# Hybrid SSD/GLA decoder trunk on one core: projecting z of two groups, and values of two heads, in one pass 512 columns wide

## The chip, the core and the metric

The kernel runs on one core of a Trainium2 chip. The core has a matrix engine (TensorE, in the profile PE; its loads of stationary operands are PEld), a vector engine (VectorE, DVE), an activation engine (ScalarE, ACT), a general engine (GpSimd, POOL) and SyncE (SP), which here only issues transfers. Matrix products land in PSUM, which has eight banks; a bank holds 128 rows of 512 float32 numbers. The metric is device time in microseconds of one execution; the figure for a kernel is the median over runs.

## The reference

One decoder layer over 2048 tokens of width 1024, with 16 learned meta tokens put in front. Everything is float32.

```python
u = rmsnorm(h, norm_w)
z, xbc, dt_raw, q, k, v, g_gla, a_lr, merge_g = split_cols(u @ w_in, IN_WIDTHS)
# SSD branch: 4 groups of 4 heads, scan over chunks of 128 tokens
xbc = silu(causal_depthwise_conv(xbc))           # x, B, C
y   = ssd_chunked(x, softplus(dt_raw + dt_bias), -exp(a_log), B, C) + d_skip * x
y_ssd = rmsnorm_per_group(y * silu(z))           # z: 1024 columns, 256 per group
# GLA branch: 4 heads, keys of 128, values of 256, decay per key channel
log_a = log_sigmoid(a_lr @ gla_gate_w2 + gla_gate_b) / 16
y_gla = rmsnorm_per_head(gla_chunked(q / sqrt(128), k, v, log_a)) * silu(g_gla)
# merge
merged = sigmoid(g1) * (y_ssd @ w_branch[0]) + sigmoid(g2) * (y_gla @ w_branch[1])
out = rmsnorm(h + merged @ w_out)[:, 16:]
```

Both scans carry a state from chunk to chunk; the meta tokens' chunk sets the first state. What the change touches is the projection of z (a 2048 x 1024 product with a 1024 x 1024 matrix, then z * sigmoid(z) up to a factor) and of v (the same size).

## The kernel before

**Arithmetic.** A float32 product is made of three products of float32r operands: each operand is split into a high part and a rest, and `accum` (L183 to L187) issues high x high, high x rest and rest x high into one PSUM bank. So every product appears in the profile as three matmuls, on L185, L186 and L187.

**Stages.** The tokens are cut into four blocks of 512 (block 0 carries the 16 meta tokens too). For each block, eight units run in order: `ssd_proj` for SSD groups 0 to 3, then `gla_proj` for GLA heads 0 to 3. After the blocks come gate, branch and output products (`Stage`), which the change doesn't touch.

**Two forms of projection.** `proj_feat` puts the result's channels on the 128 rows: the stationary operand is a 128 x 128 weight tile, the moving one 512 tokens; 24 matmuls of 512 columns for 128 channels (in block 0, some go as two halves of 264). `proj_tok` puts tokens on the rows: the stationary operand is 128 tokens of `u`, the moving one a strip of weights. For z of groups 1 to 3 and for the values of each head the strip is 256 columns wide, the four token tiles of a block share two banks of the pool `pj` (`halves_of`), and the work is 96 matmuls. Group 0's z goes with the small dt and decay columns, 288 wide, in five (block 0) or four banks taken from three pools. In block 0 the values also need the meta tokens' rows, a fifth tile, in a bank of `pt`.

**PSUM.** Eight banks in three pools: `pj` 3 (projections, the gates' matmuls), `pt` 3 (transposes, sums), `pc` 2 (the scans' products). A tile is taken by `bank(pool, tag)`; if all of a pool's banks are in use, the instruction that first writes the new tile waits until the last reader of an older one is done.

**Order.** While the blocks run, the order on PE and SP is that of the program text (`manual_schedule`); the order on DVE, ACT and POOL is chosen by the framework's planner. Each projection unit is a generator. At each of its `yield`s the loop at L852 calls `step()`, which advances every running generator by one call: SSD scans (`ssd_scan`, eight calls, nine in block 0), GLA scans (`gla_scan`, eleven calls), `dt_chain`, `gates` (seven calls; it makes the GLA decays, with two matmuls on L434 in its second and fifth call), the next block's `load_u`, and a unit that adds up operands for the later products. So a block is 48 steps: a piece of projection, then one call of everything that runs beside it. A scan begins when the unit that feeds it has ended (`begin`). Before, `gates` begins with unit 1.

**In a scan's call.** An SSD call (`before`, `after`) takes a `pt` bank for three transposes, then a `pc` bank `py` and a second `pc` bank `pst`; `py` is free after L575 on DVE, `pst` after L570. A GLA scan takes two `pt` banks at once for its sums (fifth call), `pt` for transposes (second, sixth and tenth; L816 is the tenth, L817 on DVE frees its banks), `pc` banks for the products of two levels in several calls (L703, freed by L710) and for `po` in the seventh and eighth (L799 to L801, freed by L806 on ACT).

**The end of the blocks.** The last head's scan (block 3, head 3) begins as soon as its values are projected, ahead of the head's two output-gate projections, with `last=True`: it transposes its keys in its sixth call rather than the second. When the projections have run out, the loop over `k` steps the scans that are left, and puts between the steps the first work of the gate products (`between`).

Of the kernel before, what the change touches and what calls it, by code (L numbers as in the profile page):

```python
# [14 lines left out]
P = 128  # L15
D = 1024
KT = 8
META = 16
# [8 lines left out]
NT4 = 5  # L27
# [13 lines left out]
def trunk_kernel(ctx: ExitStack, tc: tile.TileContext, xm, xmt, w_feat, w_tok, w_zm, w_br, w_o,  # L41
# [303 lines left out]
    def new_block(b, u):  # L345
# [14 lines left out]
        o.alr = mk(bpool, [P, 5, 48], F32, "alr")  # L360
        o.mov = lambda kt, a, n: tuple(t[:, kt, a:a + n] for t in u)
# [3 lines left out]
    def dt_chain(o, psd):  # L365
# [12 lines left out]
        e = t80("de")  # L378
        nc.scalar.activation(e, x, AF.Abs)
        nc.scalar.activation(e, e, AF.Exp, scale=-1.0)  # L380
        w1 = t80("dw")
        nc.vector.tensor_scalar(w1, e, 1.0, None, op0=ALU.add)
        ln = t80("dl")
# [66 lines left out]
    def ssd_proj(o, g):  # L450
        m0, tt = o.m0, o.tt
        feats = []
        zs = mk(wk, [P, NCH, 256], F32, "tok4", bufs=NT4)
        if g == 0:
            pss = [bank(*pl) for pl in [(pj, "pj")] * 3 + [(pt, "pt")] + ([(pc, "pc")] if m0 else [])]
            yield from proj_tok("zm", w_zm, o.u, o.starts + [0] * o.ci0, list(enumerate(pss)), 288, 1, 256)
            begin(dt_chain(o, pss[NCH:] + pss[:NCH]))
            done = [(ps[:, :256], zs[:, c]) for c, ps in enumerate(pss[:NCH])]
# [7 lines left out]
        yield  # L466
# [138 lines left out]
    def gla_proj(o, h):  # L605
        m0 = o.m0
# [6 lines left out]
        for ps, (a, n) in zip(proj_feat(f"g{t0 + 1}", w_feat[t0 + 1], o.segs_all, o.mov), o.segs_all):  # L613
            nc.scalar.activation(kf[:, a:a + n], ps[:, :n], AF.Copy)
        yield
        vh = mk(wk, [P, NCH, 256], F32R, "tok4", bufs=NT4)
        vl = mk(wk, [P, NCH, 256], F32R, "tok4", bufs=NT4)
        vm = None
        pss, places = halves_of(pj, "pj")
        if m0:  # L620
            vm = mk(wk, [P, 256], F32, "c1", bufs=NC1)[:META]
            pv5 = bank(pt, "pt")
            places.append((2, pv5[:, :256]))
        yield from proj_tok(f"v{h}", w_tok[SG + h], o.u, o.starts + [0] * o.ci0, places)

        last, gs = (o.b, h) == (nblk - 1, GH - 1), []
        if last:
            begin(gla_scan(o, h, qs, kf, (vh, vl), vm, gs, True))
        if m0:
            nc.scalar.activation(vm, pv5[:META, :256], AF.Copy)  # L630
        for r, ps in enumerate(pss):
            split(*[t[:, 2 * r:2 * r + 2].rearrange("p c f -> p (c f)") for t in (vh, vl)], ps)
        yield
        for j in range(2):
# [6 lines left out]
        if not last:  # L641
            begin(gla_scan(o, h, qs, kf, (vh, vl), vm, gs))
# [182 lines left out]
    def begin(gen):  # L825
        begun.append(gen)
# [322 lines left out]
def _layout(inputs):  # L1149
# [26 lines left out]
    w_tok = tiles(np.concatenate([cols(o_z, 1024), cols(o_v, 1024)], axis=1), 256)  # L1176
# [34 lines left out]
    return {"xm": xm, "xmt": xmt, "w_feat": w_feat, "w_tok": w_tok, "w_zm": w_zm, "w_br": w_br, "w_o": w_o, "cf32": cf32, "cmsk": cmsk.reshape(P, -1),  # L1211
# [21 lines left out]
```

## Time and profile before

| | |
|---|---|
| median of 3 runs | 2332.01 us (2328.81, 2332.01, 2332.72) |
| profiled execution, span | 2327.3 us, granted TensorE clock 0.988 |
| PE busy | 2247.1 us (97%), 12641 matmuls |
| PEld busy | 1956.3 us (84%) |
| DVE busy | 1550.3 us (67%) |
| ACT busy | 1184.8 us (51%) |
| POOL busy | 684.6 us (29%) |
| transfers | 518.05 MB, mean 223 GB/s |

Each profile row gives start or total times of one engine, line and operation. The page gives no time of the profiled execution other than its span, from the first to the last instruction; the span is 4.7 us under the median of the runs, and sums are made against the span and carried over to the median. Matmuls are pipelined, so that their modelled durations overlap; two rows' starts tell how far apart they ran. Blocks 0 to 3 begin near 14, 416, 779 and 1141 us by their first 288-wide rows; the projections end near 1494 us, and the products after the blocks run alone from about 1550 us.

### The profile page before, as it was taken

To read this page: it belongs to the slowest core of one execution; us is meant where nothing else is said; L and a number is where in the kernel's file an instruction comes from. 1 tells how busy PE (TensorE), PEld (TensorE's weight loads), DVE (VectorE), ACT (ScalarE), POOL (GpSimd) and SP (SyncE) were. 2 spreads that over 40 slices of the span, in tenths; PEclk is the share of its full clock that TensorE was granted. 3 is DMA by queue.
4 is the path that set the end of the run, shared out by engine and by line. 5 is a ranking of instruction groups with operands and counts; after the bars stand their busy time and mean duration, and the time that the engine had idled before them with its cause. 6 is when DMAs were issued, how large, how long until landed. Compare 5 with 4: busy or idle time off the path is not lost. (4 is left out here: it accounts for less than half of the span.)

```text
span 2327.3 us, 36519 instructions
## 1 busy us (share of the span) xinstructions
PE 2247.1 (97%) x12641; PEld 1956.3 (84%) x12641; DVE 1550.3 (67%) x2895; ACT 1184.8 (51%) x2758; POOL 684.6 (29%) x681
## 2 busy tenths in 40 slices
PE   7899999999999999999999999889999999999998
PEld 7899888888888989898988898768888888888776
DVE  5676766676675666566568555654588954788766
ACT  4666655465544455544465443554554545554443
POOL 3344433122221122212122100037324264324331
PEclk9999999999999999999999999989999999999999
DMA  8766865767785666786677655457577866687743
GB/s 302 230 204 208 292 228 205 223 199 237 244 284 181 214 213 217 255 270 215 194 230 214 206 168 162 145 178 247 186 255 268 305 227 216 231 286 259 243 145 122
DMA packets 301545, 518.05 MB, mean 223 GB/s; under 512 B 27696, under 2 KB 143664, under 8 KB 301360
## 3 DMA queue, kind: packets, MB, share of 16 engines
q1 hardware_dynamic: 200400, 402.84, 53.0%
q10 hardware_dynamic: 100960, 112.88, 14.1%
q8 instruction: 99, 1.62, 0.3%
q14 instruction: 86, 0.70, 0.1%
HBM read 368.42 MB, written 147.19 MB: 222 GB/s over the span
## 5 line engine op out<-in xcount | busy, mean ns | idle before, releaser
L185 PE MATMUL pj<-u,whl 128*128 128x512 f32 (+1 forms) x1184 | 449.0, 379 | 14.6 <-ACT acc L475 6.7
L187 PE MATMUL pj<-u,whl 128*128 128x512 f32 (+1 forms) x1184 | 433.5, 366 | 1.4 <-POOL whl L166 0.8
L186 PE MATMUL pj<-u,whl 128*128 128x512 f32 (+1 forms) x1184 | 432.0, 365 | 0.0
L185 PE MATMUL pj<-whl,u 128*128 128x256 f32 (+1 forms) x992 | 289.0, 291 | 2.4 <-ACT u L298 1.5
L187 PE MATMUL pj<-whl,u 128*128 128x256 f32 (+1 forms) x992 | 282.4, 285 | 1.6 <-DVE u L300 1.6
L186 PE MATMUL pj<-whl,u 128*128 128x256 f32 (+1 forms) x992 | 282.2, 284 | 1.0 <-POOL whl L166 1.0
L185 PEld LDWEIGHTS pj<-u,whl 128*128 128x128 f32 x1184 | 226.8, 192 | 53.7 <-ACT acc L475 7.7
L185 PE MATMUL pj<-b,a 128*128 128x512 f32 x640 | 254.0, 397 | 13.8 <-ACT sn L945 7.6
L187 PEld LDWEIGHTS pj<-u,whl 128*128 128x128 f32 x1184 | 226.0, 191 | 38.0 <-POOL whl L166 1.9
L186 PEld LDWEIGHTS pj<-u,whl 128*128 128x128 f32 x1184 | 227.0, 192 | 33.6
L187 PE MATMUL pj<-b,a 128*128 128x512 f32 x640 | 252.2, 394 | 0.0
L186 PE MATMUL pj<-b,a 128*128 128x512 f32 x640 | 251.0, 392 | 0.0
L185 PEld LDWEIGHTS pj<-whl,u 128*128 128x128 f32 x992 | 189.7, 191 | 4.0 <-ACT u L298 1.8
L187 PEld LDWEIGHTS pj<-whl,u 128*128 128x128 f32 x992 | 189.6, 191 | 2.3 <-DVE u L300 2.3
L80 POOL TENSOR_TENSOR wr<-wr 128x256 f32<-128x256 f32 x80 | 66.3, 829 | 425.0 <-DMA wr<-u 174.7
L186 PEld LDWEIGHTS pj<-whl,u 128*128 128x128 f32 x992 | 189.9, 191 | 1.6 <-POOL whl L166 1.2
L166 POOL TENSOR_TENSOR whl<-wr,whl 128x512 fp32r<-128x512 f32 (+1 forms) x100 | 134.7, 1355 | 187.4 <-ACT whl L165 151.5
L904 DVE TENSOR_TENSOR b<-br,b 128x512 fp32r<-128x512 f32 x196 | 154.9, 808 | 44.7 <-ACT b L903 43.5
L919 POOL TENSOR_TENSOR as<-ar,ar 128x512 f32<-128x512 f32 x40 | 60.0, 1499 | 411.3 <-DMA ar<-in_w_br 197.3
L479 DVE SCALAR_TENSOR_TENSOR acc<-cin,hcw,acc 128x512 f32<-128x512 f32 (+1 forms) x192 | 154.4, 804 | 30.9 <-ACT acc L475 29.8
L929 DVE TENSOR_TENSOR a<-ar,a 128x512 fp32r<-128x512 f32 x160 | 126.3, 797 | 67.2 <-ACT a L928 64.4
L903 ACT ACTIVATE b<-br 128x512 fp32r<-128x512 f32 x196 | 119.4, 626 | 99.0 <-DMA br<-br_t 38.6
(274 smaller groups left out, 5068.8 us busy)
## 6 DMA issues: line engine op xcount, KB each, us to landing
whl<-k_s SPq DMA_DIRECT2D x96, 512.0 KB, 4.5
whl<-k_g SPq DMA_DIRECT2D x96, 512.0 KB, 4.2
whl<-k_v SPq DMA_DIRECT2D x48, 512.0 KB, 3.7
whl<-k_z SPq DMA_DIRECT2D x36, 512.0 KB, 3.8
wr<-in_w_feat SPq DMA_DIRECT2D x64, 256.0 KB, 4.5
k_s<-whl SPq DMA_DIRECT2D x32, 512.0 KB, 3.6
cb<-cumd ACTq DMA_DIRECT2D x64, 256.0 KB, 5.8
y<-gg ACTq DMA_DIRECT2D x64, 256.0 KB, 4.5
```

Source lines behind the costliest of these rows:

```text
L80: nc.gpsimd.tensor_tensor(o, x, y, op=ALU.subtract)
L166: nc.gpsimd.tensor_tensor(hl[:, 1], raw, hl[:, 0].bitcast(F32), op=ALU.subtract)
L185: nc.tensor.matmul(ps, sh, mh, start=first, stop=False, **kw)
L186: nc.tensor.matmul(ps, sh, ml, start=False, stop=False, **kw)
L187: nc.tensor.matmul(ps, sl, mh, start=False, stop=last, **kw)
L479: nc.vector.scalar_tensor_tensor(acc, cin[:, k:k + tt], hcw[:, ti, k:k + 1], acc, op0=ALU.mult, op1=ALU.add)
L903: nc.scalar.activation(t[:, 0], raw, AF.Copy)
L904: nc.vector.tensor_tensor(t[:, 1], raw, t[:, 0].bitcast(F32), op=ALU.subtract)
L919: nc.gpsimd.tensor_tensor(s1, a21, a22, op=ALU.add)
L929: nc.vector.tensor_tensor(t[:, 1], src, t[:, 0].bitcast(F32), op=ALU.subtract)
```

## The change

Z of groups 1 and 2 is projected in unit 1, 512 columns wide, into four banks (three of `pj`, one of `pt`); unit 2 has then no z projection. Group 3's z stays 256 wide. The values of heads 0 and 1 are projected in unit 4, those of heads 2 and 3 in unit 6, in the same way; in block 0 the meta tokens' tile takes a bank of `pc`. `proj_tok` yields after each quarter of a wide projection. The four tiles are read out 256 columns at a time, as each bank holds two groups or heads. A block still has 48 steps: the units have 6, 8, 4, 6, 8, 4, 8 and 4 of them in place of six each. `gates` begins with unit 2. The scan of heads 1 and 3 transposes its keys in the sixth call in every block. In block 3, the scan of head 2 begins after its values, then head 3's query and key are projected, its scan begins, and the output gates of both heads (four projections) come last. The weights' strips are laid out anew for this on the host (`w_pair`, `w_z3`), with as many bytes and loads as before. `tok4` gets a sixth buffer; five small tiles per block have one buffer in place of two, and `dt_chain` uses three of them as scratch; the meta tokens' values wait in the state tile `s_gla`.

```diff
-NT4 = 5
+NT4 = 6
...
         for q0 in range(0, nq, 2):
-            if q0 == nq // 2:
+            if q0 and (q0 == nq // 2 or width == 512):
                 yield
...
+    def token_banks(m0):
+        return [bank(*pl) for pl in [(pj, "pj")] * 3 + [(pt, "pt")] + ([(pc, "pc")] if m0 else [])]
...
-            setattr(o, nm, mk(bpool, [P, 5, NH], F32, nm, bufs=2))
+            setattr(o, nm, mk(bpool, [P, 5, NH], F32, nm))
...
     def ssd_proj(o, g):
...
+        elif g == 1:
+            pss = token_banks(0)
+            yield from proj_tok("z1", w_pair[0], o.u, o.starts, list(enumerate(pss)), 512, 1)
+            o.zs.update({i: mk(wk, [P, NCH, 256], F32, "tok4", bufs=NT4) for i in (1, 2)})
+            done = [(ps[:, i * 256:(i + 1) * 256], o.zs[1 + i][:, c]) for c, ps in enumerate(pss) for i in range(2)]
+        elif g == 3:
+            pss, places = halves_of(pj, "pj")
+            yield from proj_tok("z3", w_z3, o.u, o.starts, places)
+            zs = o.zs[3] = mk(wk, [P, NCH, 256], F32, "tok4", bufs=NT4)
+            done = [(ps, zs[:, 2 * r:2 * r + 2].rearrange("p c f -> p (c f)")) for r, ps in enumerate(pss)]
         else:
-            pss, places = halves_of(pj, "pj")
-            yield from proj_tok(f"z{g}", w_tok[g], o.u, o.starts, places)
-            done = [(ps, zs[:, 2 * r:2 * r + 2].rearrange("p c f -> p (c f)")) for r, ps in enumerate(pss)]
+            done = []
+        zs = o.zs[g]
         for ps, dst in done:
             nc.scalar.activation(dst, ps, AF.Tanh, scale=0.5)
             nc.vector.scalar_tensor_tensor(dst, dst, 1.0, ps, op0=ALU.add, op1=ALU.mult)
-        yield
+        if done:
+            yield
...
+    def gla_values(o, h):
+        m0 = o.m0
+        vs = [[mk(wk, [P, NCH, 256], F32R, "tok4", bufs=NT4) for _ in range(2)] for _ in range(2)]
+        vms = [s_gla[:META, h + i] for i in range(2)]
+        pss = token_banks(m0)
+        yield from proj_tok(f"v{h}", w_pair[1 + h // 2], o.u, o.starts + [0] * o.ci0, list(enumerate(pss)), 512, 1)
+        for c, ps in enumerate(pss[:NCH]):
+            for (vh, vl), i in zip(vs, range(2)):
+                split(vh[:, c], vl[:, c], ps[:, i * 256:(i + 1) * 256])
+        for i in range(2):
+            if m0:
+                nc.scalar.activation(vms[i], pss[NCH][:META, i * 256:(i + 1) * 256], AF.Copy)
+            o.vals[h + i] = vs[i], vms[i]
+        yield
...
+    def gla_proj(o, h):
+        end = o.b == nblk - 1 and h >= GH - 2
+        gs = o.gs.setdefault(h, [])
+        if not end or h == GH - 2:
+            yield from gla_keys(o, h)
+        if h % 2 == 0:
+            yield from gla_values(o, h)
+        if end and h == GH - 2:
+            begin(gla_scan(o, h, *o.gla[h], *o.vals[h], gs))
+            yield from gla_keys(o, h + 1)
+            begin(gla_scan(o, h + 1, *o.gla[h + 1], *o.vals[h + 1], o.gs.setdefault(h + 1, []), True))
+        yield from gla_out_gates(o, h, o.gs[h])
+        if not end:
+            begin(gla_scan(o, h, *o.gla[h], *o.vals[h], gs, h % 2 == 1))
...
-            if i == 1:
+            if i == 2:
                 begin(gates(o))
```

`gla_keys` (query and key projections, two steps) and `gla_out_gates` (two output-gate projections, two steps) are the parts of the old `gla_proj` under names of their own.

More of the change, by code (lines that the diff above doesn't have):

```diff
@@ L614, in gla_proj, with gla_out_gates @@
             nc.scalar.activation(kf[:, a:a + n], ps[:, :n], AF.Copy)
+        o.gla[h] = [qs, kf]
         yield
[L616 to L632, printed above, removed]
+    def gla_values(o, h):
+        m0 = o.m0
+        vs = [[mk(wk, [P, NCH, 256], F32R, "tok4", bufs=NT4) for _ in range(2)] for _ in range(2)]
+        vms = [s_gla[:META, h + i] for i in range(2)]
+        pss = token_banks(m0)
+        yield from proj_tok(f"v{h}", w_pair[1 + h // 2], o.u, o.starts + [0] * o.ci0, list(enumerate(pss)), 512, 1)
[6 more added lines that the diff above has]
+            o.vals[h + i] = vs[i], vms[i]
         yield
+    def gla_out_gates(o, h, gs):
+        t0 = T_GLA + 4 * h
         for j in range(2):
@@ L1175, in _layout @@
     w_feat = tiles(np.concatenate(feat, axis=1), P)
[L1176 removed]
+    w_pair = tiles(np.concatenate([cols(o_z + 256, 512), cols(o_v, 1024)], axis=1), 512)
+    w_z3 = tiles(cols(o_z + 768, 256), 256)[0]
     wb = np.asarray(inputs["w_branch"])[0]
```

21 lines of the change are left out of this document (9 added, 12 removed).

## The prediction

> **What bounds the kernel now.** I read the page's busy times, then the starts of single matmuls in the timeline, then PE's waits, then the stretch in which the blocks end. The page:
>
> ```profile
> span 2327.3 us, 36519 instructions
> PE 2247.1 (97%) x12641; PEld 1956.3 (84%) x12641; DVE 1550.3 (67%) x2895; ACT 1184.8 (51%) x2758; POOL 684.6 (29%) x681
> ```
>
> PE is the bound, and nearly without holes. The groups by line and shape name the matmuls at stake (narrow, with `u` stationary) and the wide ones whose form is nearest:
>
> ```profile
> L186 PE MATMUL pj<-u,whl 128*128 128x512 f32 x864 | 338.1, 391 | 0.0
> L186 PE MATMUL pj<-whl,u 128*128 128x256 f32 x896 | 253.0, 282 | 1.0 <-POOL whl L166 1.0
> ```
>
> The mean durations, 282 and 391 ns, are no prices, since matmuls overlap. The price is the distance of starts. The timeline, first a narrow run, then a wide one, then one of group 0 (288 columns):
>
> ```profile
> 1078.13 0.28 PE L186 MATMUL pj<-whl,u 128*128 128x256 f32 x1
> ...
> 1081.85 0.28 PE L187 MATMUL pj<-whl,u 128*128 128x256 f32 x1
> ...
> 1062.84 0.40 PE L186 MATMUL pj<-u,whl 128*128 128x512 f32 x1
> ...
> 1067.85 0.39 PE L187 MATMUL pj<-u,whl 128*128 128x512 f32 x1
> ...
> 424.86 0.29 PE L186 MATMUL pj<-whl,u 128*128 128x288 f32 x1
> ...
> 426.56 0.29 PE L187 MATMUL pj<-whl,u 128*128 128x288 f32 x1
> ```
>
> 31 intervals in 3.72 us are 120 ns; 22 in 5.01 us are 228 ns; 13 in 1.70 us are 131 ns. So 256 columns more cost 108 ns, and each matmul carries some 12 ns whatever its width.
>
> PE's waits over the whole run are short. Three of the largest (total us, times, longest), the two on `pj` among them:
>
> ```profile
> PE pt L790 <- DVE sq L781: 6.8, 2, 4.4
> PE pj L185 <- ACT acc L475: 6.7, 5, 4.3
> PE pj L185 <- ACT g_all L437: 4.4, 2, 3.1
> ```
>
> The PSUM pools as they are used now thus hardly hold PE up. That is what the change touches.
>
> **Term 1, the wide projections.** Z: 4 blocks x 4 tiles x 8 slices x 3 = 384 wide matmuls; values: 2 pairs x 4 blocks x 96, and 24 more per pair in block 0 for the meta tile = 816. 1200 wide ones replace 2400 narrow ones: 1200 x (2 x 120 - 228) = 14.4 us less. All of it lies on PE, so it counts in full. Bounds: 0 (a wide one costs two narrow ones) and 1200 x 12 ns = 14.4, the value I take, since both widths are measured and the 288-wide run has the new form's operands.
>
> The Trainium skill, "TensorE: Matmul & The Clock Gate", section "Back-to-back issue gap", gives an isolated warm gap of the width over 2.4 GHz plus 2.5 ns; by it term 1 is an estimate of 1200 x 2.5 ns = 3 us, and my sum would come out some 11 us later. The rows above disagree (120 ns for 256 columns, where it has 109), and the rows decide.
>
> **Edits costed at nothing.** The evacuation today (ACT, then DVE, 512 columns), a DVE product of 256, and a load with its time to landing:
>
> ```profile
> L464 ACT ACTIVATE tok<-pj 128x512 f32<-128x512 f32 x24 | 14.1, 589 | 18.1 <-PE pj L187 17.9
> L465 DVE SCALAR_TENSOR_TENSOR tok<-tok,pj 128x512 f32<-128x512 f32 x24 | 16.5, 686 | 39.3 <-ACT tok L464 39.2
> L577 DVE TENSOR_TENSOR tok<-c,tok 128x256 f32<-128x256 f32 x64 | 29.8, 466 | 1.2
> whl<-k_g SPq DMA_DIRECT2D x96, 512.0 KB, 4.2
> ```
>
> Reading out in 256s has twice as many and shorter instructions: a 512-wide tanh is 589 ns; of DVE's products a 512-wide is 686 and a 256-wide 466. Eight of 466 for four of 686 are 1.0 us more per pair on DVE, and about as much on ACT, which are at 67% and 51%. The loads are as many, of the same size and in the program's order on SP, in steps of the same length; a load lands after some 4.2 us and four `whl` buffers lie ahead. ACT's own transfers keep their number. The four moved output gates take their eight weight loads with them, behind head 3's query and key on SP. The small tiles' old readers (group 3's scan) end some 15 steps before the next block writes them. `tok4` with six buffers holds at most six live tiles by my count.
>
> **Term 2, the end of the blocks.** The last head's scan now begins one step earlier against the last projection, so seven of its calls lie behind it, not eight. A window of 10 us (DVE is its third busy time), the last projection's end and the wait at the end:
>
> ```profile
> 1490.00:1500.00 10.00, 8.36 (x44) 6.26 (x42) 10.00 (x29) 5.24 (x14) 0.00 (x0) 1.00 0.48 154
> ...
> 1493.98 0.61 PE L703 MATMUL pc<-sq 128*128 128x128 f32 x4
> ...
> 1543.32 1.22 PE L185 MATMUL pj<-b,a 128*128 128x512 f32 x2 [6.10 <-ACT b L903]
> ```
>
> From 1494.0 to 1543.3 are 49.3 us for eight steps, 6.2 each. One less: -6.2. It can be nothing, as DVE, full in that window, now has both scans' levels ahead of it, or twice that, if what is left of the gate products also fills the 6.1 us.
>
> **Term 3, the decays' matmuls.** `gates` begins at unit 2, so its fifth call falls into step 19, the middle of group 3's z, which holds two of the three `pj` banks open. The two matmuls on L434 (heads 2 and 3) need a bank each: the second waits until L436 and L437 have read the first, and behind it on PE stands the rest of the block. How long that takes, in block 1 where nobody waited and in block 0 where PE did; the last three rows are a wait of PE at 698 us and matmuls behind it:
>
> ```profile
> 505.81 0.72 PE L434 MATMUL pj<-act,w 48*128 48x512 f32 x2
> 508.63 0.75 DVE L436 TENSOR_SCALAR tok<-pj,pv 128x512 f32<-128x512 f32 x1
> 510.74 1.27 ACT L437 ACTIVATE g_all<-pj,pv 128x512 f32<-128x512 f32 x2 [1.47 <-DVE tok L436]
> ...
> 79.50 0.39 PE L434 MATMUL pj<-act,w 48*128 48x264 f32 x1
> 83.42 0.46 ACT L437 ACTIVATE g_all<-pj,pv 128x264 f32<-128x264 f32 x1
> ...
> 698.28 0.70 PE L801 MATMUL pc<-s_gla,act 128*128 128x256 f32 x2 [2.72 <-DVE s_gla L802]
> 699.30 0.63 PE L187 MATMUL pj<-u,whl 128*128 128x512 f32 x1
> 702.29 0.57 PE L185 MATMUL pj<-u,whl 128*128 128x512 f32 x1
> ```
>
> The floor is 0.75 on DVE and 0.64 on ACT behind it, 1.4; the top is block 0's 4.0 (79.9, the first product's end, to 83.88) and 1.4 for a slow clock behind it: after a wait of 2.7 us at 698 us seven intervals of matmuls were 427 ns each and not 228.
>
> I take the middle, 3.4, four times: 13.6, less 1.3 (4.4 - 3.1) for the second of block 0's two waits for L437, whose place goes: +12.3 (ends 4 and 20).
>
> The same page of the Trainium skill (section "What's actually happening") halves the clock after an idle window of about 3.4 us. The row at 698 shows it behind a shorter wait. By the rule alone the 1.4 would fall away at the middle value and term 3 be some 3 us less.
>
> **Term 4, one `pc` bank in block 0.** The meta tile of a values pair holds one of the two `pc` banks for four steps. In the first pair, three SSD calls need `py` and `pst` at once, and `pst` (L567) now waits for L575:
>
> ```profile
> 156.96 0.59 PE L567 MATMUL pc<-c,bt 128*128 128x256 f32 x2
> 158.88 0.41 DVE L575 TENSOR_TENSOR c<-c,pc 128x256 f32<-128x256 f32 x1
> ...
> 262.48 0.59 PE L567 MATMUL pc<-c,bt 128*128 128x256 f32 x2
> 265.78 0.41 DVE L575 TENSOR_TENSOR c<-c,pc 128x256 f32<-128x256 f32 x1
> ...
> 334.63 0.59 PE L801 MATMUL pc<-s_gla,act 128*128 128x256 f32 x2
> 336.06 0.38 ACT L806 ACTIVATE junk<-pc 128x256 bf16<-128x256 f32 x1
> ```
>
> 2.3 us (156.96 to 159.29) or 3.7 (262.48 to 266.19); the middle, 3.0, three times: 9. In the second pair, head 0's `po` and head 1's levels share the one bank: four waits behind a `po` of some 1.4 (334.9 to 336.44, a part hidden) and three between levels of some 0.7 (DVE's 466 ns for 256 columns and a start on either side): 7.7. Sum +16.7 (ends 7 and 24). Block 0's projections have little slack to swallow this; a values step there had PE busy throughout:
>
> ```profile
> 337.20:355.10 17.90, 17.90 (x150) 17.37 (x148) 8.23 (x19) 8.68 (x20) 5.35 (x5) 1.00 0.40 133
> ```
>
> **Term 5, two `pt` banks.** Each pair holds one. Where it ends, two scans' transposes meet: z's pair with the last block's head 3 (three blocks), values' second pair with heads 0 and 1 (four). The third request waits for the first L817:
>
> ```profile
> 1083.77 1.04 PE L816 MATMUL pt<-cst,ot 128*128 128x128 f32 x8
> 1084.40 0.75 DVE L817 SCALAR_TENSOR_TENSOR gg<-pt,hgw,gg 128x512 f32<-128x512 f32 x1 [1.65 <-PE pt L816]
> ...
> 494.84 0.93 PE L816 MATMUL pt<-cst,ot 128*128 128x128 f32 x7
> 496.95 1.40 DVE L817 SCALAR_TENSOR_TENSOR gg<-pt,hgw,gg 128x512 f32<-128x512 f32 x2
> ```
>
> 0.5 us (1084.64 to 1085.15) to 2.0; nearest the former, 0.7 x 7: +5 (ends 0 and 14).
>
> **Sum.** -14.4 - 6.2 + 12.3 + 16.7 + 5 = +13.4 on a span of 2327.3; carried to the median of 2332.0 (4.7 above the span): 2345.
>
> **Rivals.**
>
> The banks come back at once. The planner may put the read-out of a bank that PE waits for ahead of all else. Place: terms 3 to 5. Price: term 3 at its floor less what block 0 loses now, 5.6 - 4.4 = 1; term 4 at 7; term 5 at 0. Then 2332 - 20.6 + 8 = 2319. For it: DVE and ACT have a third and a half free, and the longest pool wait quoted above is 4.3. Against: when PE stood for L437 at 79.9, the bank still took 4.0. It decides when the new waits sum to under 20.6 - 4.7 = 16 us.
>
> DVE becomes the bound in units 2 and 3. Without z's evacuation steps the gates' calls and two groups' scans meet feature steps. The third step after group 1's z, where the like happens today:
>
> ```profile
> 497.50:506.50 9.00, 8.79 (x44) 6.78 (x42) 9.00 (x24) 4.38 (x12) 1.41 (x3) 1.00 0.62 212
> ```
>
> DVE is full for one step and PE loses little. Two more such steps per block, each 2 us over, are 15 us: 2360.
>
> The end grows instead. Both last scans use the one buffer `ot`, two steps apart; head 3's copies wait for head 2's transposes, and term 2 turns to about +4: 2355.
>
> Width buys nothing: 240 ns for 512 columns with `u` stationary, 2345 + 14.4 = 2359; the 288-wide run speaks against it. The skill's rule above leads nearly there.
>
> The durations are prices after all: 1200 x (2 x 282 - 391) = 208 us less, 2124. The starts exclude it.
>
> **How the numbers follow.** 0.2% (4.7 us) is about what a measurement here tells from no change. Forecast 2345: 0.46, of which 0.09 lies within 0.2%. Banks at once, 2319: 0.29, of which 0.04 within. DVE bound 0.10, longer end 0.08, no width gain 0.05, all slower; durations 0.02. Faster 0.25 + 0.02 = 0.27; same 0.13; slower 0.37 + 0.23 = 0.60. The forecast's own range, 2332 to 2358, has the middles of its terms. For eight in ten: low 2309 (the first rival with term 2 doubled and a little over), high 2368 (terms 3 and 4 near their ends).
>
> **What would show it.** Right: 512-wide `pj<-whl,u` starts 228 ns apart; PE waits of 1.4 to 5 us on L434 for L437 once per block; in block 0 waits of L567 for L575 and of L799 to L801 for L806; blocks 1 and 2 about as long as now (363 and 362 us between the starts named ahead), block 0 well over its 402; from the last projection to the first wait for L903 some 43 us. Wrong: L434's waits under 1.5 us, or block 0 no longer than now.

## The result

The changed kernel took 2422.95 us, the median of runs from 2420.45 to 2430.18, against 2331.18 us for the kernel before (one run more than in the table above): a ratio of 1.040, 95% interval 1.0382 to 1.0418. The prediction was 2345, with 2368 as its upper end; the direction was right, the size was far off. The profiled execution has a span of 2428.4 us.

The first two rows of the page of the kernel after, to be held against the two of before:

```profile
span 2428.4 us, 34235 instructions
PE 2277.7 (94%) x11441; PEld 1918.7 (79%) x11441; DVE 1559.6 (64%) x2943; ACT 1194.1 (49%) x2806; POOL 677.0 (28%) x681
```

PE issues 1200 matmuls fewer, and yet its span grew by 101.1 us (2428.4 - 2327.3). Its share of busy time fell from 97% to 94%: the engine that was nearly without holes now waits, and is slower around the waits, as the granted clock says (0.971 for the whole run, 0.988 before). PE idles 150.7 us (2428.4 - 2277.7) where it idled 80.2 (2327.3 - 2247.1): 70.5 more. The lower clock takes up to 42 us more (0.029 of 2428.4 us against 0.012 of 2327.3), an estimate that has PE busy throughout. Less the 14.4 us of width, the two make some 98 of the 101. PE's waits of the kernel after (total us, times, longest):

```profile
PE pc L728 <- ACT junk L831: 12.5, 8, 3.3
PE pc L536 <- DVE s_ssd L582: 11.7, 2, 7.8
PE pj L436 <- ACT g_all L439: 11.0, 4, 3.2
...
PE pc L728 <- DVE c L735: 7.3, 11, 1.2
PE pt L749 <- DVE gg L842: 6.7, 5, 2.4
PE pc L579 <- DVE c L587: 6.5, 2, 3.4
PE pc L728 <- DVE s_gla L762: 5.3, 2, 4.8
```

Every row shown names a PSUM pool. L728 is the product of two levels of a GLA scan (L703 before), L831 the last reader of a `po` bank (L806), L436 and L439 the decays' matmul and reader (L434, L437), L536 the scores at the start of an SSD scan (L524), L579, L582 and L587 the `pst` product and the readers of `pst` and `py` (L567, L570, L575), L749 the turning of the keys. The prediction had priced L436 in every block, and L579, the first and the fourth row in block 0 alone. It had nothing for L536, and nothing for levels that wait for `po` in blocks 1 to 3, where 11 of the first row's 12.5 us lie.

The timeline of the kernel after shows where blocks 1 to 3 begin (288 columns), where the last projection ends, and between 898.98 and 902.17 fourteen intervals of wide matmuls of z:

```profile
451.89 0.38 PE L185 MATMUL pj<-whl,u 128*128 128x288 f32 x1
...
835.25 0.38 PE L185 MATMUL pj<-whl,u 128*128 128x288 f32 x1
...
898.98 0.39 PE L186 MATMUL pj<-whl,u 128*128 128x512 f32 x1
...
902.17 0.39 PE L185 MATMUL pj<-whl,u 128*128 128x512 f32 x1
...
1222.61 0.38 PE L185 MATMUL pj<-whl,u 128*128 128x288 f32 x1
...
1601.16 0.39 PE L187 MATMUL pj<-u,whl 128*128 128x512 f32 x1
```

The blocks take 437, 383, 387 and 379 us (block 0 begins at 14.4) where they took 402, 363, 362 and 353: 35, 20, 25 and 26 more. The loss isn't mostly block 0's, as the prediction had it (blocks 1 and 2 about as long as now); each block has 20 us of it or more. The wide matmuls stand 3.19 / 14 = 228 ns apart, as predicted.

### The profile page after: what moved, and what is told of

Read it like the earlier page. It is cut to its first block, busy times and chain, and to the rows that moved or that the text cites. A ratio compares the mean times of both kernels' runs of the same rounds, so it can differ in the third digit from the quotient of the medians.

```text
span 2428.4 us, 34235 instructions
## 1 busy us (share of the span) xinstructions
PE 2277.7 (94%) x11441; PEld 1918.7 (79%) x11441; DVE 1559.6 (64%) x2943; ACT 1194.1 (49%) x2806; POOL 677.0 (28%) x681
## 3 DMA queue, kind: packets, MB, share of 16 engines
q8 instruction: 90, 1.47, 0.2%
## 5 line engine op out<-in xcount | busy, mean ns | idle before, releaser
L185 PEld LDWEIGHTS pj<-u,whl 128*128 128x128 f32 x1184 | 229.8, 194 | 48.0 <-ACT g_all L439 3.8
L187 PEld LDWEIGHTS pj<-u,whl 128*128 128x128 f32 x1184 | 228.0, 193 | 39.2 <-POOL whl L166 2.1
L186 PEld LDWEIGHTS pj<-u,whl 128*128 128x128 f32 x1184 | 229.1, 194 | 34.2
L185 PE MATMUL pj<-whl,u 128*128 128x512 f32 (+2 forms) x512 | 191.5, 374 | 3.5 <-DMA whl<-k_zm 1.7
L187 PE MATMUL pj<-whl,u 128*128 128x512 f32 (+2 forms) x512 | 182.7, 357 | 1.5 <-DVE u L301 1.4
L186 PE MATMUL pj<-whl,u 128*128 128x512 f32 (+2 forms) x512 | 182.9, 357 | 0.8 <-POOL whl L166 0.8
L928 ACT ACTIVATE b<-br 128x512 fp32r<-128x512 f32 x196 | 120.2, 627 | 102.2 <-DMA br<-br_t 36.8
L185 PEld LDWEIGHTS pj<-b,a 128*128 128x128 f32 x640 | 121.3, 190 | 37.8 <-ACT sn L970 9.7
L186 PEld LDWEIGHTS pj<-b,a 128*128 128x128 f32 x640 | 121.4, 190 | 29.0 <-DVE b L929 2.2
L187 PEld LDWEIGHTS pj<-b,a 128*128 128x128 f32 x640 | 121.2, 189 | 27.7
```

Source lines behind the costliest of these rows:

```text
L185: nc.tensor.matmul(ps, sh, mh, start=first, stop=False, **kw)
L186: nc.tensor.matmul(ps, sh, ml, start=False, stop=False, **kw)
L187: nc.tensor.matmul(ps, sl, mh, start=False, stop=last, **kw)
L928: nc.scalar.activation(t[:, 0], raw, AF.Copy)
```

## The experiments

Line numbers differ by kernel: in those that change values only, L529, L572, L575 and L580 are the score, the `pst` product and the readers of `pst` and `py`, L721 the levels' product and L824 the last reader of `po`. Ratios are to the kernel before, with 95% intervals.

### Two halves

The change was first cut at its seam: one kernel with z and `gates` of the change and values, scans and end as before; one with the values, scans and end of the change and z and `gates` as before.

```diff
 z alone (wide z, gates at unit 2):
-            yield from gla_values(o, h)            # pairs
+        yield from proj_tok(f"v{h}", w_v[h], ...)  # per head, as before
 values alone:
-            yield from proj_tok("z1", w_pair[0], ..., 512, 1)
+            yield from proj_tok(f"z{g}", w_z3[g], ...)   # per group
...
-            if i == 2:
+            if i == 1:
                 begin(gates(o))
```

The text on z alone calls "the run with z alone" a kernel that comes further below, wide z with the gates at unit 3 (2345.7 us).

> As the run with z alone, but the gates begin at unit 2 as in the change, so their fifth call meets the two banks of group 3's z. Theory: this meeting alone costs 20 to 24 us (what the later gates gave back in the full change), 2348 to 2354 us. By the prediction's term 3 (3.4 us a block and one clock loss) it costs 12: 2339 to 2343. Rival (the gates' place matters only beside the wide values): within 5 us of the run with gates at unit 3.

> Values as in the change, both scans of a pair behind their gates, four and eight steps apart; z and gates as before. Same matmuls as the run with early scans at 2340.3. Theory (level products of the second scan meet the four po banks of the first on the two pc banks, twice a block): about 40 us over that run, 2375 to 2385, spread over all blocks. Rival (the spacing only matters where late gates push the scans together): 2340 to 2355.

Z alone took 2369.4 us (1.0157, 1.0137 to 1.0176), 38 more than the kernel before it ran beside; values alone 2384.4 us (1.0224, 1.0201 to 1.0248), 54 more. Values alone lie in the range expected; z alone lies 15 us above the highest of its three. The sum of 92 is the whole loss (2422.95 - 2331.18 = 92). So the two halves don't need each other, and each can be taken apart alone.

### The spacing of the scans

In the change a GLA scan begins when its unit ends, and the units of heads 0 to 3 have eight, four, eight and four steps. Two scans of a pair so run four steps apart, where all ran six apart. The seventh and eighth call of the first, which take four `po` banks, then fall on the third and fourth of the second, which take banks for the levels' products; all come from the two banks of `pc`. The edit lets the even heads' scans begin right behind their values, six steps ahead of the next. It also puts the turning of the keys of heads 1 and 3 back from the sixth call into the second. It was tried in the full change, in the full change with `gates` begun at unit 3, and with values alone:

```diff
         if h % 2 == 0:
             yield from gla_values(o, h)
+            if not end:
+                begin(gla_scan(o, h, *o.gla[h], *o.vals[h], gs))
...
-        if not end:
-            begin(gla_scan(o, h, *o.gla[h], *o.vals[h], gs, h % 2 == 1))
+        if not end and h % 2:
+            begin(gla_scan(o, h, *o.gla[h], *o.vals[h], gs))
```

> The changed kernel with the scans of heads 0 and 2 begun right behind their values and ahead of the output gates, and no late turning of keys for heads 1 and 3: the GLA scans of one block then follow each other six steps apart, as before the change, and not four and eight. Theory of banks: the seventh and eighth call of one scan (four po banks) no longer meet the third and fourth of the next (levels, L728) on the two pc banks, and the waits of L728 for L831 and L735 and the slow clock behind them go: 15 to 20 us per block, some 2360 us. Rival, that the overlap of scans costs DVE and ACT time and not banks: less than 20 us are gained, as the number of calls per step is the same on the mean.

> Both edits together. Theory of banks: the two places are apart and their gains add up; what is left of the change is its 14 us from width and its shorter end against one pc bank less in block 0 and one pt bank less beside each pair: 2315 to 2335 us. Rival (one overload, moved about): the gains do not add, and the time stays above 2360.

> z and gates as before the change; values of two heads 512 wide, scans of even heads begun behind their values, so six steps apart. Theory: nearly all of the 24 us that are left with late gates and early scans are the values', and most of these block 0's one pc bank: 2352 to 2360 us, blocks 1 and 2 within 5 us of 363 and 362, block 0 15 to 20 us over 402. Rival (wide form costs everywhere): 2345 to 2350, the loss spread over all blocks alike.

The full change with early scans took 2384.5 us (1.0227), 38 less than without; with late gates too 2355.2 (1.0100, 1.0076 to 1.0124) against 2398.7 for late gates alone, 44 less; values alone 2340.3 (1.0034, 1.0024 to 1.0045) against 2384.4, 44 less. In the last pair the matmuls are the same in number and form, so the spacing, with the turning of the keys that went with it, costs 44 us, more than the prediction's sum of losses. PE's waits for the turning (L742 for L835) are 6.8 us of values alone and none with early scans. No run has one without the other, so that part of the 44 isn't told apart. The expectations went wide: the first kernel gained 38 us where 60 was expected, the second came out between its two ranges, the third below both. The two steps in which they meet, in block 2 (windows: us, then busy us of PE, PEld, DVE, ACT, POOL, the granted clock, DMA share, GB/s); first values alone, four apart, then six apart:

```profile
830.40:844.40 14.00, 10.68 (x55) 9.19 (x54) 10.73 (x36) 9.52 (x27) 3.72 (x5) 0.89 0.72 233
844.40:856.80 12.40, 11.62 (x55) 9.40 (x54) 6.42 (x15) 4.66 (x13) 0.19 (x1) 0.85 0.27 85
```

```profile
812.00:818.80 6.80, 6.80 (x39) 5.82 (x38) 5.27 (x16) 5.57 (x14) 3.85 (x5) 1.00 0.65 224
818.80:826.50 7.70, 7.70 (x47) 6.60 (x46) 7.08 (x18) 5.29 (x13) 1.23 (x3) 1.00 0.70 208
```

26.4 us against 14.5; the two steps ahead have fewer calls in the first kernel and take 14.4 there against 18.4, so this meeting costs 8 net. Heads 0 and 1 meet in the values steps of heads 2 and 3, heads 2 and 3 in the next block's steps 3 and 4. The second place costs more: in block 1 of values alone PE's waits on `pc` are 5.3 us there (467.32 and 481.48) and 2.7 in the values steps (745.18 to 758.08). The loss lies in all blocks, as the theory had it: 11, 13, 13 and 10 us from block 0 to 3 (values alone 425.7, 376.1, 373.1 and 367.8; with early scans 414.5, 363.5, 360.4 and 357.4). In the first kernel's timelines of PE and ACT the wait and its cause stand side by side:

```profile
841.88 2.07 PE L721 MATMUL pc<-sq 128*128 128x128 f32 x8 [3.32 <-ACT junk L824]
```

```profile
838.71 0.42 ACT L234 ACTIVATE c<-c 128x256 fp32r<-128x256 f32 x1 [1.27 <-DVE tkd L390]
839.14 1.28 ACT L709 ACT_TABLE_LOAD   x1
840.44 0.44 ACT L709 ACTIVATE sq<-sq 128x256 f32<-128x256 f32 x1
...
841.36 0.38 ACT L824 ACTIVATE junk<-pc 128x256 bf16<-128x256 f32 x1
```

ACT serves its instructions in the planner's order: it waits 1.27 us for another chain, changes its table (1.28), makes the exponentials of a level, and only behind these reads `po`. PE stands for 3.32 us with the levels' product, and the next projection behind it. The bank is held not as long as its reader runs (0.38) but as long as the work ahead of the reader takes. That `pc` is what makes the spacing cost is read from these rows; no run gives `pc` a third bank.

### Block 0, its one `pc` bank, and the end

With early scans, values alone still lose 9 us. Two edits look for them: the meta tile of the values pair in a `pt` bank and not in `pc` (in the full change with both repairs), and block 0's values head by head as before, wide ones in blocks 1 to 3 alone, whose strips are then loaded by two transfers. A third takes only the new end into the kernel before, with narrow values.

```diff
 meta tile on pt:
-        return [bank(*pl) for pl in [(pj, "pj")] * 3 + [(pt, "pt")] + ([(pc, "pc")] if m0 else [])]
+        return [bank(*pl) for pl in [(pj, "pj")] * 3 + [(pt, "pt")] + ([(pt, "pt")] if m0 else [])]
 narrow in block 0:
+            ... (gla_proj if b else gla_proj0)(o, i - SG)   # gla_proj0: as before the change
```

> Late gates and early scans, and in block 0 the meta tile of a values pair lies in the second pt bank, so the level products, py and pst have both pc banks. Theory: the waits on pc in block 0 (L579 and L529 for L587, 11 us) go, but for four steps the transposes have no pt bank beside; 8 to 15 us less than 2355: 2340 to 2347. Rival 1: the transposes' wait takes their place, 2353 to 2362. Rival 2 (block 0 is longer for other reasons, such as the meta matmuls' own form): 2353 to 2357 with block 0 as long as now, 420 us.

> Values of two heads 512 wide with early scans in blocks 1 to 3, and in block 0 narrow, head by head, as before; z as before. Theory: what v_early lost (2340.3, 9 over before) was all in block 0, whose length goes back from 414 to 402: 2340 - 12.5 = 2326 to 2329, that is before less the 3 x 192 x 12 ns = 6.9 us of width (the end moves nothing) and some loss on pt: faster by 0.1 to 0.3%. Rival (block 0's extra time is only moved, or the wide values load by two transfers of 256 KB that come late): 2333 to 2340.

> The kernel before with the end of block 3 alone changed: query, key and values of heads 2 and 3, each scan begun behind its values, then the four output gates. If the end is worth what the prediction took, some 6 us less than the kernel before (2325); if the one buffer ot makes it longer, some 4 us more; if it is nothing, within 3 us.

The meta tile on `pt` gave 2349.1 us (1.0068, 1.0051 to 1.0084), 6 less than 2355.2 (the two intervals just overlap) and between its expectations. Yet block 0 of that kernel takes 418.0 us against 419.8 with the tile on `pc` (first 288-wide starts at 14.3 and 432.3, and at 14.5 and 434.3), as its second rival said. The waits for `py` (5.9 us) went, and others came in block 0 from 230 us on: 2.4 us for a `pt` bank (L611) and 2.3 more for the weights' split (L165). Narrow values in block 0 gave 2325.5 us (0.9972, 0.9958 to 0.9986), faster than the kernel before. So what values alone still lost, and 14 us in all (from 1.0034 to 0.9972 of 2331), was block 0's. Its place is the four steps of the first pair of values; windows of values alone with early scans, then of the two heads' values in the kernel before (19.4 + 19.3 us):

```profile
235.40:246.50 11.10, 9.11 (x43) 6.66 (x40) 5.71 (x10) 11.10 (x35) 4.88 (x4) 1.00 0.71 269
246.50:259.30 12.80, 9.51 (x46) 7.66 (x46) 8.99 (x17) 6.59 (x15) 6.48 (x6) 0.94 0.96 350
259.30:276.00 16.70, 13.26 (x55) 10.80 (x54) 6.44 (x14) 3.28 (x9) 3.24 (x3) 0.81 0.30 106
276.00:286.50 10.50, 10.30 (x48) 8.23 (x47) 7.33 (x16) 6.29 (x16) 2.11 (x2) 0.89 0.48 163
```

```profile
235.70:255.10 19.40, 18.44 (x149) 17.50 (x147) 11.58 (x20) 16.47 (x45) 9.28 (x9) 1.00 0.89 313
285.50:304.80 19.30, 18.20 (x149) 17.30 (x148) 14.05 (x23) 10.19 (x24) 6.79 (x5) 1.00 0.83 285
```

51.1 us against 38.7. The first kernel's PE waits there for `py` in the one `pc` bank, twice:

```profile
258.68 1.19 PE L572 MATMUL pc<-c,bt 128*128 128x256 f32 x2 [3.29 <-DVE c L580]
...
274.18 0.67 PE L572 MATMUL pc<-c,bt 128*128 128x256 f32 x2 [3.44 <-DVE c L580]
```

The waits are 6.7 us of the 12.4; the lower clock (0.94, 0.81 and 0.89 in the last three windows) can make up to 5.1 of the 5.7 that are left, an estimate with PE busy throughout (12.8 x 0.06 + 16.7 x 0.19 + 10.5 x 0.11).

The new end alone took 2330.0 us (0.9995, 0.9981 to 1.0010): no change. Its profile says why. The blocks' projections end at 1508.5 us there and at 1493.9 before, 14.5 later, and from there to the last instruction it is 820 us and not 833, 13 less: what the end saves behind the last projection it had spent ahead of it.

### z and the gates

In eight kernels `gates` begins elsewhere, or takes its banks from `pt`, or stands beside a narrow z:

```diff
 gates at unit 3 (full change; wide z alone; narrow z), at unit 2 and 1 (narrow z):
-            if i == 2:
+            if i == 3:
                 begin(gates(o))
 decays' matmuls in pt (wide z; gates at unit 2 and at unit 1):
-                    ps = bank(*((pt, "pt") if i else (pj, "pj")))
+                    ps = bank(pt, "pt")
 gates right behind the wide z, in unit 1:
+                if (i, n) == (1, 3):
+                    begin(gates(o))
```

> The changed kernel with one number altered: the decays' generator begins with unit 3, not unit 2. Its two matmul calls then fall behind group 3's z and between two feature projections, as they fell around group 1's z before the change. Theory of banks: steps 19 and 20 of a block, which took 27 to 29 us against some 16 without waits, lose their 11 to 14 us in each of four blocks: some 2378 us. Rival, that DVE and ACT are overloaded in this stretch whatever the order: the same work waits elsewhere, and the time stays within 10 us of 2423.

> Only z of groups 1 and 2 is projected 512 wide, and the gates begin at unit 3; values, scans and the end are as before the change. If losses come from banks that interleaved scans share (theory), this has none but the single pt bank where the last block's transposes meet it: 384 wide matmuls x 12 ns = 4.6 us gained, up to 2 lost on pt, 2327 to 2331 us. If the wide form itself costs (rival: read-out in 256s, six live tok4 tiles, loads), z pays its share of the 24 us that are left when gates begin at unit 3 and the scans start early: 8 us, 2339.

> All projections narrow and all scans, gates and the end as before the change; only the small tiles are single and tok4 has six buffers. The prediction costed these at nothing: 2328 to 2335 us, the kernel before within its scatter. Rival: the single tiles make block b+1's decay chain wait for block b's last scan, 1 to 3 us a block more, 2336 or over.

> As the run with small tiles alone, and the gates begin at unit 2. Group 2's z is here a step sequence of its own, so the gates' fifth call falls behind it and not between the two halves of group 3's z. Theory (it is the meeting on the three pj banks that costs, not the later start): within 5 us of the run with gates at unit 1. Rival (any later start costs, as the scans of head 0 and the gates crowd together): 10 us or more above it.

> As the run with small tiles alone, and the gates begin at unit 3, z narrow. z of two groups with gates at unit 3 took 2345.7 us, 14 more than before. If the wide z makes that (read-out in 256s, group 3's scan meeting the first head), this run is within 5 us of the run with gates at unit 1; if the late gates make it, it is at 2343 to 2349.

> z of two groups wide, gates begin at unit 2, all else as before the change; the decays' matmuls take their banks from pt and not from pj, so their fifth call no longer needs a bank beside the two that group 3's z holds. With pj this was 2369.4, and with narrow z and gates at unit 2 2334.6. Theory (the shared pj banks make the 35 us): 2328 to 2337, the 4.6 us of width gained over the narrow run and some of it lost on pt. Rival (the fifth call and z's second half in one step crowd DVE and ACT, whichever bank): over 2355.

> As the run with the decays in pt, and the gates begin at unit 1 as before the change, though the wide z holds all three pj banks and one pt bank for four steps. Theory: later gates cost 5 us a unit (2328.8, 2334.6, 2343.7 with narrow z), so this is 2322 to 2330. Rival: with one pt bank left for gates and transposes in these steps the wait only moves to pt, 2335 to 2350.

> z of two groups wide, the gates begin right behind its four steps in unit 1 (not at unit 2), decays in pj as in the change, all else as before. The run with the decays in pt (2373.3) showed that it isn't the pj banks: there DVE is full where the decays' scans meet group 2's last convolutions and group 3's z, and puts them ahead of the products that free pc. Theory: five steps earlier the same six calls meet feature steps alone: 2326 to 2338 (narrow z with gates one unit late had 2334.6, less 4.6 for the width). Rival (two groups' z read out at once crowd DVE wherever the gates stand): 2343 or more, as with gates at unit 3 (2345.7).

Measured, as z alone; the full change with gates at unit 3 took 2398.7 (1.0288), 24 less than at unit 2:

| gates begin | z narrow | z wide, decays in `pj` | z wide, decays in `pt` |
|---|---|---|---|
| unit 1 | 2328.8 (0.9999, 0.9983 to 1.0015) | | 2377.4 (1.0196, 1.0178 to 1.0214) |
| behind the wide z, unit 1 | | 2358.3 (1.0128, 1.0113 to 1.0144) | |
| unit 2 | 2334.6 (1.0015, 1.0002 to 1.0029) | 2369.4 (1.0157, 1.0137 to 1.0176) | 2373.3 (1.0180, 1.0159 to 1.0200) |
| unit 3 | 2343.7 (1.0053, 1.0037 to 1.0070) | 2345.7 (1.0064, 1.0040 to 1.0089) | |

The small tiles cost nothing (2328.8). The full change with gates at unit 3 lies between its two expectations; wide z with gates at unit 3 lies above both of its own, and the narrow run beside it says why. A later start of the gates costs by itself, 6 us for one unit (hardly clear of the intervals) and 15 for two; with two, PE waits 8.1 us for weight strips, where it waits 1.2 with the gates at unit 1 (waits of the two kernels, gates at unit 3 first):

```profile
PE pj L185 <- DMA whl<-k_g: 8.1, 2, 4.2
```

```profile
PE pj L185 <- DMA whl<-k_g: 1.2, 2, 0.7
```

The prediction had costed the loads at nothing. With wide z and the gates at unit 2, 33 us come on top (38.0 over the kernel before on its chip, narrow z 4.7). And my theory for these, the `pj` bank that the fifth call lacks, fell: with the decays in `pt` the time was no less. The waits of z alone and of the kernel with the decays in `pt` show what happened:

```profile
PE pj L436 <- ACT g_all L439: 10.8, 4, 3.2
...
PE pc L536 <- DVE s_ssd L582: 8.3, 1, 8.3
...
PE pc L536 <- DVE c L587: 5.3, 3, 3.0
```

```profile
PE pc L536 <- DVE s_ssd L582: 31.4, 4, 8.2
```

The wait for a bank of `pj`, 3.2 us a block, went away, and the wait of L536 on `pc` grew from 13.6 us in all (8.3 and 5.3) to 31.4, up to 8.2 in a block: L536, the start of group 3's scan, which follows group 3's z, waits for the last `pst` of group 2. In z alone the rows of L436 and L536 make 24.4 of the 38 us; the lower clock of its profiled execution (0.980 of 2364.8 us, 0.988 of 2327.3 before) can make up to 19 more, an estimate as above, and the width gives 4.6 back. The timeline of DVE at that place, decays in `pt`:

```profile
575.85 1.29 DVE L445 TENSOR_TENSOR tok<-tok,g_all 128x512 f32<-128x512 f32 x2 [3.02 <-ACT g_all L442]
577.76 0.69 DVE L476 SCALAR_TENSOR_TENSOR tok<-tok,pj 128x512 f32<-128x512 f32 x1 [0.62 <-ACT tok L475]
578.37 1.05 DVE L447 TENSOR_TENSOR_SCAN g_all<-ones_r,tok 128x128 f32<-128x128 f32 x3
579.33 0.40 DVE L584 TENSOR_TENSOR c<-pc,ecu 128x256 f32<-128x256 f32 x1
579.65 3.65 DVE L447 TENSOR_TENSOR_SCAN g_all<-ones_r,tok 128x128 f32<-128x128 f32 x5
583.22 0.39 DVE L582 TENSOR_TENSOR s_ssd<-s_ssd,pc 128x256 f32<-128x256 f32 x1
```

DVE waits 3.02 us for the decays' logarithms, then runs eight scans of them (4.7 us), and only between and behind these the two readers that free `pc` (L584, L582, 0.4 us each). In the kernel after, the same two steps of block 2 (windows, columns as above) have DVE busy almost without a break in the first, and the granted clock at 0.77 in the second:

```profile
980.50:994.00 13.50, 9.26 (x67) 8.13 (x65) 13.46 (x30) 6.24 (x16) 3.65 (x6) 1.00 0.40 146
994.00:1008.00 14.00, 11.61 (x72) 11.11 (x72) 8.58 (x20) 9.23 (x19) 1.35 (x2) 0.77 0.35 114
```

PE's timeline has two waits there: the one that the prediction had priced, and 12 us later one of L536 for the reader of group 2's last `py`, which no term had. Behind each the matmuls run at about half their rate: 13 intervals in 2.78 us are 214 ns for 256 columns, not 120, and 3 in 1.28 are 427 for 512, not 228:

```profile
993.65 0.50 PE L436 MATMUL pj<-act,w 48*128 48x512 f32 x1 [3.19 <-ACT g_all L439]
...
995.13 0.41 PE L186 MATMUL pj<-whl,u 128*128 128x256 f32 x1
...
997.91 0.41 PE L187 MATMUL pj<-whl,u 128*128 128x256 f32 x1
...
1005.73 2.05 PE L536 MATMUL pc<-act,act 128*128 128x128 f32 x8 [2.39 <-DVE c L587]
...
1008.64 0.63 PE L186 MATMUL pj<-u,whl 128*128 128x512 f32 x1
...
1009.92 0.63 PE L186 MATMUL pj<-u,whl 128*128 128x512 f32 x1
```

By these traces the cause at unit 2 is that three chains meet on DVE and ACT: group 2's last products, the gates' fifth and sixth call, and group 3's z. Which bank PE then stands for depends on the pool that the decays take; that it stands did not, in these two kernels. No run takes work off DVE or ACT there, so this is read from the traces and not shown by an experiment. With the gates at unit 1 beside the wide z, the time (2377.4) is above both expectations, and the wait is again another, for the reader of an SSD scan's transposes on `pt`:

```profile
PE pt L436 <- ACT bt L561: 14.1, 4, 3.6
```

The kernel with the gates right behind the wide z was to show the reverse, in steps where that meeting can't be (four steps earlier than at unit 2, by the loop). It came out on the rival's side (2343 or more): it is 29 us over the kernel before, not 38; so 9 came back, and it is still 24 above narrow z with gates at unit 2 (4.7). Its largest wait has moved again:

```profile
PE pj L185 <- ACT acc L487: 20.1, 15, 3.8
```

L487 reads a feature projection out of `pj` on ACT; the kernel before has the like at 6.7 us, nearly all in block 0, and of the 20.1 some 11 lie in blocks 1 to 3. Wide z thus costs beside the gates at every place tried, save where they begin after it is all used up (unit 3, where wide and narrow z can't be told apart, so that the read-out in 256s and the loads cost no more than the width gives, within the intervals). That ACT, which now evacuates two groups at once and serves the gates, is the whole reason at that place was not tried by taking ACT's work away, and stays open.

### Together

Two kernels join the wide values of blocks 1 to 3 with wide z: one with the decays in `pt` and the gates at unit 1, one with the gates right behind the wide z.

> Wide values in blocks 1 to 3 with early scans, narrow in block 0; wide z with gates at unit 1 and the decays in pt. If the parts add up: 2325.5 plus what z with gates at unit 1 and decays in pt gains or loses by itself; by theory 2318 to 2324, faster than before by 0.3 to 0.5%. Rival: pt, now needed by gates, transposes and both pairs, is short: 2330 or more.

> Wide values in blocks 1 to 3 with early scans (narrow in block 0, alone 2325.5 at 2329.9 before, so -4.4), and wide z with the gates right behind it. If the parts add up, this stands at before - 4.4 plus what the run with z alone gains or loses: by theory 2320 to 2333; by the rival 2338 or more.

They took 2368.0 us (1.0147, 1.0125 to 1.0170) and 2350.9 us (1.0094, 1.0076 to 1.0111), both on the rival's side. By the parts it would be 1.96 - 0.28 = 1.68% and 1.28 - 0.28 = 1.00% over the kernel before; it is 1.47 and 0.94. The parts add up within the intervals, and no form of wide z tried is worth having. The version that beats both kernels is the one with wide values in blocks 1 to 3, narrow ones in block 0, early scans, and z and gates as before: 2325.5 us, 0.9972 of the kernel before.

## Why the prediction was wrong

The step that failed is the account of what the change does to waits for banks: it counted the banks that the change itself takes, put the new spacing of the scans at nothing, and priced the gates' new place by one wait. The runs showed 44 us for the spacing and 38 for z with its gates, where the sum had 0 and 12.3.

- **Term 1, the width (-14.4).** Right as a price: 228 ns in the rows above, and the kernel with 576 wide matmuls in blocks 1 to 3 should gain 576 x 12 ns = 6.9 us and gained 6.5 (0.28%, interval 0.14 to 0.42). The rival that width buys nothing is out.
- **Term 2, the end (-6.2).** The stretch behind the last projection did shrink, from 833 to 827 us in the kernel after, and the first wait for L928 (L903 before) ended at 1641.6, 40 us behind it, where 43 was said. But the end by itself is worth nothing (0.9995): the term counted the side behind the last projection alone, and the steps ahead of it grew by as much.
- **Term 3, the gates' fifth call (+12.3).** The step was right in place, once in each block, and in the wait (3.2 us where 3.4 was taken). It was wrong in what it costs: 33 us and not 12, and 5 more for the later start. There are two waits and not one, for L436 and, in the next step, for L536 (10.8 and 13.6 us in z alone), with a slow clock behind both; and with the decays in `pt` the first went and the second grew, so the one wait wasn't the price. In the first of the two steps DVE is busy 13.46 us of 13.50, and the rival "DVE becomes the bound in units 2 and 3" named this mechanism and this place, with 2 us a step and a chance of 0.10. In the second DVE isn't full (8.58 of 14.00); there the banks' readers stand behind the decays' scans, and these behind ACT's logarithms. How the 33 us are shared between the two stays open.
- **Term 4, block 0's one `pc` bank (+16.7).** Near in size: 14 us, and 240 wide matmuls x 12 ns = 2.9 that block 0 would have gained, 16.9. The waits of L567 for L575 are there, 3.29 and 3.44 us where 3.0 was taken, twice and not three times, and 12.4 us lie in the first pair. But with the meta tile on `pt` these waits are gone and block 0 is hardly shorter (418.0 against 419.8), so that it needs the one `pc` bank to be this long isn't shown, and the size is in part luck.
- **Term 5, `pt` (+5).** The waits for L842 (L817 before) come to 11.5 us, between the term's ends of 0 and 14, but mostly not where it put them. Where z's pair meets the last block's head 3, they are 0.4 each, 1.2 in all, near the smaller price (0.5). The rest, 6.7 and 3.6, stands in the sixth call of a scan (L749 and L815), which at four steps apart meets the tenth of the scan ahead: in values alone with early scans no such wait is left, so this too belongs to the spacing and the late turning of the keys.
- **What no term had (+44).** The prediction's account of `pc` stopped at block 0, since it asked which tiles the change adds to a pool. It didn't ask which calls the change puts side by side. "A block still has 48 steps" is true, but the starts of the scans moved from six and six to four and eight, and the largest loss follows from these two numbers. It could have been read beforehand: the units' steps (eight and four), the calls that take `pc` (third and fourth, seventh and eighth), and two banks. Among PE's waits before there already was a small row of levels behind `po`, which the prediction doesn't show:

```profile
PE pc L703 <- ACT junk L806: 3.7, 2, 2.6
```

The lower clock, too, has a price in term 3 alone (1.4 us a wait at its top end), where by the estimate above it is up to 42 us of the loss.

By the sum: 44 (spacing), 9 (values with early scans: block 0's 14 and what the width gives back elsewhere), and 38 (z with its gates) make 91 of the 92 measured. Of the "wrong" signs the prediction listed, none came; blocks 1 and 2, which should have stayed near 363 and 362 us, are the sign that a term was missing.

## What to carry to other kernels

When a change regroups work that is stepped in lockstep, write down for each step which calls of which chains now fall together and how many banks of each pool they need; counting what the change itself takes finds only half. In these runs a wait for a bank cost what stood ahead of its reader on the reader's engine, and where that engine was full in the step, giving the waiter another bank moved the wait. Price the slow clock behind a wait as well. And a shorter end is worth something only if the same work doesn't come back ahead of it.

## What the hardware showed that was not expected

The granted clock fell behind waits of PE that are short. Behind the wait of 3.19 us (993.65 in the kernel after) and behind the one of 2.39 (1005.73) the matmuls ran at about half their rate in the rows above, and the 0.77 of that window is both together. In the two windows of block 0 with the waits of 3.29 and 3.44 us, and in the one behind them, the clock is 0.94, 0.81 and 0.89. The wait of 3.32 us in values alone stands by itself: the windows with it and behind it have 0.89 and 0.85, and where the spacing is undone the same steps have 1.00. By an estimate with PE busy throughout, the two windows lose up to 3.4 us to the clock (14.00 x 0.11 + 12.40 x 0.15), as much as the wait itself.

The Trainium skill, "TensorE: Matmul & The Clock Gate", section "What's actually happening", has the clock halved after at least one idle window of about 3.4 us; the waits of 2.39, 3.19, 3.29 and 3.32 us are shorter than that, as is the one of 2.72 us in the prediction's row at 698, so here the measured rows decide. It doesn't happen every time: behind a wait of 2.95 us that ends at 1064.26 in the kernel after, the clock is 1.00 up to 1070. No run here shows from which length a slow clock has to be reckoned with.
